# Both projections of a hybrid encoder layer: seven products of quarter matrices in place of eight

## The chip, the cores and the metric

The kernel runs on one core of a Trainium2 chip. The metric is the device time of one execution in microseconds (us). The matrix engine (TensorE) is called PE below, the vector engine DVE, the activation engine ACT, GpSimd POOL, and SP is the engine that issues the DMAs. A bare "512-column matmul" is one instruction with 128 contraction rows, 128 output rows and 512 output columns.

## The reference: what is computed

One layer over 2048 tokens of width 1024. Every row of x is normalised and multiplied by one input matrix of 3348 columns; four branches use slices of the result; their outputs (4 x 256 channels) go through a 1024 x 1024 output matrix, are added to x, and are normalised again.

```python
h = _rmsnorm(x, norm_w[layer])
proj = h @ w_in[layer]                       # [2048, 1024] @ [1024, 3348]
(a_h, a_b, a_c, a_z, g_q, g_k, g_v, g_lr, g_z, p_u, p_z, s_z, s_xbc, s_dt) = jnp.split(proj, split_idx, axis=-1)
y_a = _conv_mixer(a_h, a_b, a_c, a_z, ...)   # b * conv3(c * h) * silu(z)
y_b = _gla_mixer(g_q, g_k, g_v, g_lr, g_z, ...)   # gated linear attention, chunks of 64
y_c = _pool_mixer(p_u, p_z, ...)             # window means of 2, 4, 8, 16 tokens, gated
y_d = _ssd_mixer(s_xbc, s_dt, s_z, ...)      # conv4 + silu on xs, B, C, then a chunked state recurrence
mix = jnp.concatenate([y_a, y_b, y_c, y_d], axis=-1)
x = x + mix @ w_out[layer]                   # [2048, 1024] @ [1024, 1024]
return _rmsnorm(x, final_norm_w)
```

All of it is fp32. Both kernels split every fp32 operand into a rounded high part and the rest as a low part (`split`: the high part a copy on ACT, the low part a subtraction on DVE), and every product is the sum of three matmuls: high by low, high by high, low by high.

## The kernel before, in words

The tokens go in two segments of 1024, each in two halves of 512. The activations lie channel-major in SBUF (`hT[f]`, 8 tiles of 128 channels by 512 tokens for half f, high and low). Weights come in blocks: `load_w` loads a block of 128 columns by 1024 channels on SP's queue and splits it as one 128x1024 copy and one 128x1024 subtraction. `block_ch` then multiplies it with one half: `mm3` issues 8 x 3 = 24 matmuls of 512 columns into one PSUM bank. Two blocks are made token-major, 128 tokens to a bank: "kv" (values, gate ranks and time steps, 276 columns) and the gates "z" (512 columns). In segment 0 kv is made by `kv_outer`, which takes the 8 channel tiles as they arrive for four banks at a time; all else token-major by `block_tok`.

The program is one list of calls. `step` is called behind every block: it emits what `later` has queued, and advances `chunk_loop`, the chunked recurrence of two branches, by half a token tile. So the small work of a branch lies between the large blocks of the next. Per segment the order is: kv and q, B, k, xs, C (convolution and silu on DVE and ACT), then `conv_a` (four pairs of blocks) with `chunk_loop` beside it, the gates z, and the pool branch (`pool_u`, `pool_z`).

In segment 0 nothing waits for the rows' 1/rms: the products take x * norm_w, and `evac` multiplies by the rows' 1/rms (`rb`, L208, spread along the free axis by a way through DRAM, `rd`, L207) when a block leaves PSUM. Segment 1's rows are scaled when they are prepared (`prep`, L252), its 1/rms is made by `row_scale` (L229 to 237) in the middle of segment 0. The mixed outputs go to DRAM (`yd`). The last phase goes through 16 token tiles: `load_y` loads one and splits it, `project` makes 2 x 24 matmuls against the output matrix, which stays in SBUF, adds x (L785) and squares (L786), `emit` scales and stores (L796).

POOL does next to nothing before: memsets and the four small DMAs to `rd`.

```python
def mm3(o, ops):                                   # L183
    for i, (lh, ll, rh, rl) in enumerate(ops):
        pe.matmul(o, lhsT=lh, rhs=rl, start=i == 0, stop=False)
        pe.matmul(o, lhsT=lh, rhs=rh, start=False, stop=False)
        pe.matmul(o, lhsT=ll, rhs=rh, start=False, stop=i == last)
def evac(s, f, dst, o, scale=None):                # L210
    if s == 0 and scale is None:
        vec.tensor_tensor(dst, o, rb[:, f, :], ALU.mult)
```

Of the kernel before, what the change touches and what calls it, by code (L numbers as in the profile page):

```python
# [20 lines left out]
KD = D // P  # L21
CH = 64
# [7 lines left out]
NWARM = 4  # L30
WINS = (2, 4, 8, 16)

KVN = 276
KVK = (3, 3, 2)
# [3 lines left out]
BLOCKS = ([('q', 0), ('B', 0), ('B', 1), ('k', 0), ('xs', 0), ('xs', 1), ('C', 0), ('C', 1)]  # L38
          + [(n, j) for j in range(2) for n in ('a_h', 'a_c', 'a_b', 'a_z')]
          + [('p_z', j) for j in range(2)])  # L40
NBLK = len(BLOCKS)

# columns of the packed per-channel parameters
PC = {}
_n = 0
for _name, _w in (('caw', 6), ('psc', 2), ('scw', 24), ('scb', 6), ('gnw', 1), ('snw', 2),
                  ('dtb', 4), ('alog', 4), ('dsk', 4), ('iw', 2), ('icnt', 32), ('hm', 4), ('ind', 2), ('id', P), ('msk', P)):
    PC[_name] = _n
    _n += _w
# [4 lines left out]
def tile_hybrid_trunk(ctx: ExitStack, tc: tile.TileContext, xtok, xT, wkv, wch, wpu, wz, wo, pw_, nw, par, gw, fnw, out):  # L54
    nc = tc.nc
    vec, act, pe, sp = nc.vector, nc.scalar, nc.tensor, nc.sync

    cp = ctx.enter_context(tc.tile_pool(name="cp", bufs=1))
    pbig = ctx.enter_context(tc.tile_pool(name="pbig", bufs=2))
    pw = ctx.enter_context(tc.tile_pool(name="pw", bufs=4))  # L60
    px = ctx.enter_context(tc.tile_pool(name="px", bufs=2))
    pseg = ctx.enter_context(tc.tile_pool(name="pseg", bufs=1))
    pg = ctx.enter_context(tc.tile_pool(name="pg", bufs=9))
    psm = ctx.enter_context(tc.tile_pool(name="psm", bufs=2))
    dr = ctx.enter_context(tc.tile_pool(name="dr", bufs=1, space=DRAM))
# [34 lines left out]
    nc.gpsimd.memset(ones, 1.0)  # L100
# [9 lines left out]
    for t in (halo_x, halo_u, halo_p, sg):  # L110
        nc.gpsimd.memset(t, 0.0)
    sd0 = psm.tile([P, 256], F32, tag="sd", name="sd0", bufs=2)
    nc.gpsimd.memset(sd0, 0.0)
    state = dict(sd=sd0)

    yd = dr.tile([SEQ // P, P, KD, P], F32, name="yd")
    rd = dr.tile([4, HALF], F32, name="rd")
    wd = dr.tile([2, P, D], F32, name="wd")

# [1 line left out]
    def rsqrt(ssq, inv, n, v=None):  # L121
        """1/sqrt(ssq*inv + EPS) of a [128, n] tile (or 1/sqrt(v)), times RS"""
# [20 lines left out]
    def load_w(src, n):  # L143
        """one packed weight tile [128, n] in its two parts"""
        raw = pw.tile([P, 1024], F32, tag="raw", name=nm("raw"), bufs=3)[:, :n]
        sp.dma_start(raw, src)
        return split_w(raw, n)

    def split_w(raw, n):
        hi = pw.tile([P, 1024], F32R, tag="wh", name=nm("wh"))[:, :n]  # L150
        lo = pw.tile([P, 1024], F32R, tag="wl", name=nm("wl"))[:, :n]
        split(raw, hi, lo)
        return hi, lo

    def fold_pu(j):
        """p_u's projection block j with the pool's channel mixing folded into it, to wd"""
        raw = px.tile([P, KD, P], F32, tag="xT", name=nm("raw"))
        wt_ = px.tile([P, 1024], F32, tag="xT", name=nm("raw"))
        sp.dma_start(wt_, wpu[j])
        mix = gen()[:, :P]  # L160
        sp.dma_start(mix, pw_[j])

        def fold(hf):
            tp = tr()
            for i in range(4):
                k = hf * 4 + i
                pe.matmul(tp[:, i * P:(i + 1) * P], lhsT=wt_[:, k * P:(k + 1) * P],  # L167
                          rhs=mix, start=True, stop=True)
            act.copy(raw[:, hf * 4:hf * 4 + 4, :], tp.rearrange("p (a b) -> p a b", a=4))
            if hf:  # L170
                sp.dma_start(wd[j], raw.rearrange("p a b -> p (a b)"))
        later(1, lambda: fold(0))
        later(2, lambda: fold(1))

    def load_kv(tiles):
        ws = []
        for i in tiles:
            k0, n = sum(KVK[:i]), KVK[i]
            w = load_w(wkv[:, k0 * KVN:(k0 + n) * KVN], n * KVN)
            ws += [(w[0][:, c * KVN:(c + 1) * KVN], w[1][:, c * KVN:(c + 1) * KVN]) for c in range(n)]  # L180
        return ws

    def mm3(o, ops):  # L183
        """o = sum of lhsT^T rhs over (lh, ll, rh, rl), each product in its three parts"""
        last = len(ops) - 1
        for i, (lh, ll, rh, rl) in enumerate(ops):
            pe.matmul(o, lhsT=lh, rhs=rl, start=i == 0, stop=False)  # L187
            pe.matmul(o, lhsT=lh, rhs=rh, start=False, stop=False)  # L188
            pe.matmul(o, lhsT=ll, rhs=rh, start=False, stop=i == last)  # L189

    hT = {}

    def big(f):
        return (pbig.tile([P, KD, HALF], F32R, tag=f"big{f}", name=nm("bh")),
                pbig.tile([P, KD, HALF], F32R, tag=f"big{f}", name=nm("bl")))

    def square_sums(xs, ssq):
        for j, xk in enumerate(xs):
            act.activation(xk, xk, AF.Square, accum_out=ssq[:, j:j + 1])  # L199

    def scale_first(f, xs):
# [688 lines left out]
```

## Time and profile before

| what | value |
|---|---|
| time, median of 3 runs | 844.27 us (844.14 to 845.06) |
| span of the profiled execution | 844.6 us |
| PE busy | 816.5 us, 97% of the span, 4272 matmuls |
| DVE busy | 499.3 us, 59%, 1253 instructions |
| ACT busy | 275.4 us, 33% |
| POOL busy | 6.3 us, 1%, 22 instructions |
| chain that ended last, by engine | PE 86%, DMA 8%, DVE 2%, ACT 2% |
| DMA | 86.71 MB, mean 103 GB/s |

The span runs from the first to the last instruction of one profiled execution, and lies 0.3 us over the median of the timed runs. A busy time adds the durations of an engine's instructions, overlaps counted once. PE's matmuls are pipelined: the duration that a matmul shows is longer than the step from one start to the next, so that a sum of work is better made from starts than from durations. The chain that ended last is followed back from the last instruction through what released each step.

### The profile page before, as it was taken

How to read it: one execution, taken by the hardware profiler on the slowest of the kernel's cores; microseconds unless marked ns; L12 is line 12 of the kernel's file. 1: busy time of each engine (PE TensorE's matmuls, PEld its weight loads, DVE VectorE, ACT ScalarE, POOL GpSimd, SP SyncE). 2: the span in 40 equal slices, each digit the busy share in tenths (PEclk: the TensorE clock that was granted, in tenths of full speed). 3: DMA queues.
4: the chain of work that ended last, by engine and by line, in shares of the span. 5: the costliest groups of instructions: out<-in, count | busy, mean ns of one | idle time of the engine just before them, and what ended most of it. 6: DMA issues, size and time to landing. Idle time of an engine off the chain costs nothing.

```text
span 844.6 us, 11158 instructions
## 1 busy us (share of the span) xinstructions
PE 816.5 (97%) x4272; PEld 675.4 (80%) x4272; DVE 499.3 (59%) x1253; ACT 275.4 (33%) x487; POOL 6.3 (1%) x22
## 2 busy tenths in 40 slices
PE   7975999999999999999999999999999999999996
PEld 6954888787878888998888787878888888888885
DVE  5545757674754588955846464544578765555544
ACT  5633444242212332355545211213334332122211
POOL 0000000000000000000000000000000000000000
PEclk9987999999999999999999999999999999999999
DMA  8664101144741033523011102111045654443221
GB/s 283 231 158 115 47 29 51 51 148 119 117 135 38 26 116 113 190 61 125 26 51 50 50 27 75 45 44 38 25 162 165 181 191 151 150 150 124 101 100 50
DMA packets 38836, 86.71 MB, mean 103 GB/s; under 512 B 3872, under 2 KB 17536, under 8 KB 38784
## 3 DMA queue, kind: packets, MB, share of 16 engines
q1 hardware_dynamic: 38656, 86.00, 32.4%
q8 instruction: 33, 0.54, 0.3%
q14 instruction: 19, 0.16, 0.1%
q0 software_dynamic: 128, 0.01, 0.0%
HBM read 68.16 MB, written 17.83 MB: 102 GB/s over the span
## 4 chain that ended last, share of the span: by engine, by line
PE 86%; DMA 8%; DVE 2%; ACT 2%; issue 1%; SPq 1%; DVEq 0%; ACTq 0%
PE acc L187 27%; PE acc L189 27%; PE acc L188 27%; DMA xtok<-in_xtok 3%; DMA rd<-rt 2%; PE up L391 1%; PE tr L638 1%; PE oy L399 1%; PE oy L403 1%; DMA rb<-rd 1%; DMA xT<-in_xT 1%; DMA xk<-in_xtok 1%; ACT xtok L199 1%; DMA raw<-in_wkv 1%; PE tr L167 0%
## 5 line engine op out<-in xcount | busy, mean ns | idle before, releaser
L187 PE MATMUL acc<-bl,wh 128*128 128x512 f32 x640 | 255.6, 399 | 6.1 <-DVE nv L127 6.1
L189 PE MATMUL acc<-bh,wl 128*128 128x512 f32 x640 | 251.3, 393 | 0.0
L188 PE MATMUL acc<-bh,wh 128*128 128x512 f32 x640 | 251.1, 392 | 0.0
L187 PEld LDWEIGHTS acc<-bl,wh 128*128 128x128 f32 x640 | 121.3, 190 | 31.9 <-issue 6.3
L189 PEld LDWEIGHTS acc<-bh,wl 128*128 128x128 f32 x640 | 121.1, 189 | 26.0
L188 PEld LDWEIGHTS acc<-bh,wh 128*128 128x128 f32 x640 | 121.4, 190 | 23.9
L188 PE MATMUL acc<-bh,yh 128*128 128x512 f32 (+1 forms) x264 | 101.0, 383 | 0.0
L189 PE MATMUL acc<-bh,yl 128*128 128x512 f32 (+1 forms) x264 | 101.0, 383 | 0.0
L187 PE MATMUL acc<-bl,yh 128*128 128x512 f32 (+1 forms) x264 | 101.0, 383 | 0.0
L140 ACT CAST wh<-raw 128x1024 fp32r<-128x1024 f32 (+3 forms) x57 | 55.9, 982 | 119.6 <-PE acc L188 106.1
L141 DVE TENSOR_TENSOR wl<-raw,wh 128x1024 fp32r<-128x1024 f32 (+3 forms) x57 | 64.5, 1135 | 36.9 <-ACT wh L140 33.6
L187 PE MATMUL acc<-wl,bh 128*128 128x512 f32 (+1 forms) x192 | 69.0, 359 | 0.0
L189 PE MATMUL acc<-wh,bl 128*128 128x512 f32 (+1 forms) x192 | 68.5, 357 | 0.0
L188 PE MATMUL acc<-wh,bh 128*128 128x512 f32 (+1 forms) x192 | 68.4, 356 | 0.0
L376 DVE SCALAR_TENSOR_TENSOR g<-g,prm,g 128x512 f32<-128x512 f32 x72 | 53.7, 751 | 8.2 <-ACT g L374 6.7
L189 PEld LDWEIGHTS acc<-bh,yl 128*128 128x128 f32 x264 | 49.6, 188 | 9.7
L188 PEld LDWEIGHTS acc<-bh,yh 128*128 128x128 f32 x264 | 49.6, 188 | 9.7
L187 PEld LDWEIGHTS acc<-bl,yh 128*128 128x128 f32 x264 | 49.6, 188 | 9.7
L785 DVE TENSOR_TENSOR r<-acc,xk 128x512 f32<-128x512 f32 (+1 forms) x33 | 22.3, 675 | 56.2 <-PE acc L189 55.0
L786 ACT ACTIVATE xk<-r 128x512 f32<-128x512 f32 (+1 forms) x33 | 20.4, 618 | 86.8 <-issue 66.6
L187 PEld LDWEIGHTS acc<-wl,bh 128*128 128x128 f32 x192 | 36.1, 188 | 5.3 <-issue 0.3
L189 PEld LDWEIGHTS acc<-wh,bl 128*128 128x128 f32 x192 | 36.1, 188 | 5.2
(191 smaller groups left out, 872.8 us busy)
## 6 DMA issues: line engine op xcount, KB each, us to landing
raw<-in_wch SPq DMA_DIRECT2D x36, 512.0 KB, 3.4
xk<-in_xtok SPq DMA_DIRECT2D x24, 512.0 KB, 3.6
yr<-yd SPq DMA_DIRECT2D x16, 512.0 KB, 4.2
out<-ot SPq DMA_DIRECT2D x30, 256.0 KB, 2.2
xT<-in_xT SPq DMA_DIRECT2D x14, 512.0 KB, 4.4
xtok<-in_xtok SPq DMA_DIRECT2D x8, 512.0 KB, 6.4
raw<-in_wz SPq DMA_DIRECT2D x8, 512.0 KB, 3.9
yd<-g SPq DMA_DIRECT2D x16, 256.0 KB, 2.8
```

What stands on the lines that cost most here:

```text
L140: act.copy(hi, raw)
L141: vec.tensor_sub(lo, raw, hi.bitcast(F32))
L187: pe.matmul(o, lhsT=lh, rhs=rl, start=i == 0, stop=False)
L188: pe.matmul(o, lhsT=lh, rhs=rh, start=False, stop=False)
L189: pe.matmul(o, lhsT=ll, rhs=rh, start=False, stop=i == last)
L199: act.activation(xk, xk, AF.Square, accum_out=ssq[:, j:j + 1])
L376: vec.scalar_tensor_tensor(t, xin[:, k:k + 512], pcol('scw', 4 * i + k), t, ALU.mult, ALU.add)
L391: pe.matmul(o[:, CH + g * P:CH + (g + 1) * P], lhsT=bt[r, tt, g, :], rhs=wxs[r, tt, g * P:(g + 1) * P], start=True, stop=True)
L399: pe.matmul(oy[rows[i], 0:256], lhsT=q[:, tok[i]], rhs=st[i][0], start=True, stop=True)
L403: pe.matmul(oy[rows[i], 256 + g * P:256 + (g + 1) * P], lhsT=cc[:, g, tok[i]], rhs=st[i][1][:, gs], start=True, stop=True)
L785: vec.tensor_tensor(r[:, cs], o, xk[:, cs], ALU.add)
L786: act.activation(xk[:, cs], r[:, cs], AF.Square, accum_out=sq[:, i:i + 1])
```

## The change

It applies Strassen's identity in Winograd's form to both large products. Two blocks of 128 weight columns (a "pair") are taken with both halves of the tokens: the weights as a 2 x 2 matrix of quarters (two blocks by two halves of the 1024 channels), the activations as a 2 x 2 matrix of quarters (two halves of the channels by two halves of the tokens). Seven products of quarters replace eight. Every product of quarters is 4 channel tiles x 3 parts = 12 matmuls of 512 columns (`mm12`), a pair 84 (`pair7`), where it was 4 blocks x 24 = 96.

- **Weights.** `prep7` loads a pair's four quarters (128x512), makes four sums on POOL, and splits seven (ACT copy, DVE subtraction). It runs one pair ahead, a step at each `tick` of the pair before.
- **Activations.** `quarters` makes seven quarter matrices `H` of each segment: b11, b21, b22, and t1 to t4, which come from four differences each 128x2048 (`diff_quarters`), and splits them. Since the identity mixes the halves, the rows' 1/rms can't be left for the evacuation: in segment 0 `quarters` first multiplies all four quarters by `rb`.
- **Evacuation.** A pair's four results come from four banks: one ACT copy and five DVE additions with a PSUM operand. Products 3, 5 and 6 are accumulated on top of another in PSUM.
- **What stays as it was by count:** kv (now k by k in both segments, `outer4`) and the gates z; z moves from behind the pairs to ahead of them, goes to DRAM (`szd`) and is read back in `gate_outputs`.
- **Moved to POOL:** in `chunk_loop` the scaling of xs by the step weights, by `dsk`, and the spreading of the state (`sb`); in the output phase three of four additions of x.
- **Order of work:** pairs qk, B, xs, C, a_h, a_c, a_b, a_z, p_u, p_z; a pair has 7 ticks; `chunk_loop` takes 3 ticks for a token tile. All of the first segment's row scales are loaded in 16 tiles of 128x512 during kv. The next segment's activations are scaled under p_u (`next_rows`), the output matrix is loaded there in segment 1. The output phase does token tiles 0 and 1 as before, and the other 14 as seven pairs.
- **Memory.** Weight tiles come from one pool of 20 tiles of 512 columns, general tiles from 10 (9 before), `acc` has 4 PSUM banks (3 before; `oy` shares `tr`'s).

```diff
+    def prep7(load, w7):
+        a11, a12, a21, a22 = [wt("wr", F32) for _ in range(4)]
+        load(a11, a12, a21, a22)
+        yield 1
+        s1 = wt("ws", F32)
+        pool.tensor_add(s1, a21, a22)
+        s2 = wt("ws", F32)
+        pool.tensor_sub(s2, s1, a11)
+        yield 1
+        w7.append(split_w(s2))
+        yield 1
+        pool.tensor_sub(a21, a11, a21)
+        w7.append(split_w(a11))
+        yield 1
+        w7.append(split_w(a21))
+        s4 = wt("ws", F32)
+        pool.tensor_sub(s4, a12, s2)
...
+    def mm12(o, w, h, start, cs=slice(0, 512)):
+        (wh, wl), (hh, hl) = w, h
+        for k in range(KH):
+            ks = slice(k * P, (k + 1) * P)
+            for i, (a, b) in enumerate(((wh, hl), (wh, hh), (wl, hh))):
+                pe.matmul(o[:, cs], lhsT=a[:, ks], rhs=b[:, k, cs], start=start and k == 0 and i == 0,
...
+    def pair7(w7, H, ev11, d12, d21, d22, done):
+        b = acc()
+        mm12(b, w7[0], H['t2'], True)
+        tick()
+        a = acc()
+        mm12(a, w7[1], H['b11'], True)
+        act.copy(d21, a)
+        vec.tensor_tensor(d12, b, d21, ALU.add)
+        tick()
+        c = acc()
+        mm12(c, w7[2], H['t3'], True)
+        vec.tensor_tensor(d22, c, d12, ALU.add)
+        tick()
+        mm12(a, w7[3], H['b21'], False)
+        ev11(a)
+        tick()
+        d = acc()
+        mm12(d, w7[4], H['t1'], True)
+        vec.tensor_tensor(d22, d, d22, ALU.add)
+        tick()
+        mm12(c, w7[5], H['t4'], False)
+        vec.tensor_tensor(d21, c, d12, ALU.add)
+        done(0)
+        tick()
+        mm12(d, w7[6], H['b22'], False)
+        vec.tensor_tensor(d12, d, d12, ALU.add)
+        done(1)
...
+    def diff_quarters(B, ks):
+        b11, b12, b21, b22 = [b[:, ks, :] for b in B]
+        vec.tensor_sub(b11, b12, b11)
+        vec.tensor_sub(b12, b22, b12)
+        vec.tensor_sub(b22, b22, b11)
+        vec.tensor_sub(b21, b21, b22)
...
+    def row_scale(hf, rt):
+        for j in range(4):
+            for h in range(2):
+                xk = gen("xk")[:, :512]
+                sp.dma_start(xk, xtok[hf * 4 + j][:, h * 512:(h + 1) * 512])
+                act.activation(xk, xk, AF.Square, accum_out=ssq[:, j, h:h + 1])
...
         def update(tt):
+            wx = psm.tile([P, 4, CH], F32, tag="wx", name=nm("wx"), bufs=2)
+            pool.tensor_tensor(wx, x4, wt_[:, tt, :].unsqueeze(2).to_broadcast([P, 4, CH]), ALU.mult)
+            pool.tensor_tensor(x4, x4, pcol('dsk', 0, 4).unsqueeze(2).to_broadcast([P, 4, CH]), ALU.mult)
...
-            vec.tensor_tensor(sb, sg.unsqueeze(1).to_broadcast([P, 4, CH]),
-                              pcol('hm', 0, 4).unsqueeze(2).to_broadcast([P, 4, CH]), ALU.mult)
+            pool.tensor_tensor(sb, sg.unsqueeze(1).to_broadcast([P, 4, CH]),
+                               pcol('hm', 0, 4).unsqueeze(2).to_broadcast([P, 4, CH]), ALU.mult)
...
+    def next_rows(s):
+        for f in range(2):
+            rb = row_scale_bc(2 * s + f)
+            for h in range(2):
+                raw = quarter(f, h)
+                for k in range(0, KH, 2):
+                    sp.dma_start(raw[:, k:k + 2, :], xT[2 * s + f, :, h * KH + k:h * KH + k + 2, :])
+                    for c in (k, k + 1):
+                        vec.scalar_tensor_tensor(raw[:, c, :], raw[:, c, :], nwt[:, h * KH + c:h * KH + c + 1], rb,
...
+        def quarters():
+            H = {}
+            if s == 0:
+                for f in range(2):
+                    rb = row_scale_bc(f)
+                    for h in range(2):
+                        for k in range(0, KH, 2):
+                            r = quarter(f, h)[:, k:k + 2, :]
+                            vec.tensor_tensor(r, r, rb.unsqueeze(1).to_broadcast([P, 2, HALF]), ALU.mult)
+                H['b11'], H['b21'] = [split_quarter(quarter(0, h)) for h in range(2)]
+                H['b22'] = split_quarter(quarter(1, 1))
+            else:
+                H['b11'], H['b21'], H['b22'] = std[0, 0], std[0, 1], std[1, 1]
...
+            for k in range(0, KH, 2):
+                diff_quarters(B, slice(k, k + 2))
+            for n, r in (('t2', B[3]), ('t3', B[1]), ('t1', B[0]), ('t4', B[2])):
+                H[n] = split_quarter(r)
...
+        for f in range(2):
+            o = [acc() for _ in range(4)]
+            if f == 1:
+                H = quarters()
+            outer4([std[f, 0], std[f, 1]], wzt, 512, o)
+            for i in range(4):
+                z = gen("z")[:, :512]
+                if i % 2:
+                    vec.tensor_copy(z, o[i])
+                else:
+                    act.copy(z, o[i])
+                sp.dma_start(szd[s * TT + f * 4 + i], z)
...
+        def done(j):
+            if j == 0:
+                for c in range(2):
+                    pool.tensor_add(r[1][c], r[1][c], xb[c])
...
+                emit(tt + 1, r2[:, 1, :], sb_)
+            else:
+                pool.tensor_add(r[0][1], r[0][1], xa[1])
...
+        pair7(w7, H, ev11, r[0][1], r[1][0], r[1][1], done)
```

How the instructions stand on three engines at the places that matter is shown below, first before and then with the change. A row is line, operation, output<-inputs, shape, and how often it stands there in a row.

**SP's queue at the start.** Before, the kv weights (`raw<-in_wkv`) stand between the activations (`xT`), and the row tiles (`xk<-in_xtok`) behind them:

```order
L528 DMA xT_163<-in_xT 128x1024
L556 DMA raw_125<-in_wkv 128x552
L528 DMA xT_173<-in_xT 128x1024
L556 DMA raw_128<-in_wkv 128x552
L146 DMA raw_183<-in_wch 128x1024
L528 DMA xT_189<-in_xT 128x1024
L539 DMA xk_196<-in_xtok 128x1024
```

With the change the last two of the eight kv tiles (`wr<-in_wkv`) stand behind both halves of the activations and among the 16 row tiles:

```order
L296 DMA xk_507<-in_xtok 128x512
L709 DMA wr_187<-in_wkv 128x276
L296 DMA xk_510<-in_xtok 128x512
L296 DMA xk_513<-in_xtok 128x512
L296 DMA xk_516<-in_xtok 128x512
L296 DMA xk_519<-in_xtok 128x512
L296 DMA xk_522<-in_xtok 128x512
L709 DMA wr_193<-in_wkv 128x276
L714 DMA wr_552<-in_wz 128x512
```

So the last kv tile, which the first four PSUM banks need, moved behind everything else that the start loads.

**DVE ahead of the first blocks of segment 0.** Before, the first channel-major block (q) leaves its bank behind one weight split:

```order
L206 TENSOR_SCALAR rt<-ny_311 128x4
L624 TENSOR_SCALAR kv_386<-kv_386,rt 128x276 x4
L141 TENSOR_TENSOR wl_573<-raw_570,wh_572 128x1024
L215 SCALAR_TENSOR_TENSOR q_388<-acc_400,rb 128x512
L127 TENSOR_SCALAR nv_365<-ssq_358 128x4
```

With the change, between the gates of the first half (`z_778`) and the first pair stand the row scaling (L792), the splits (L152) and the differences (L267 to L270) of the quarters, and behind these rows four more lines of splits, x2 each:

```order
L812 COPY z_778<-acc_603 128x512
L792 TENSOR_TENSOR xq_115<-xq_115,rb_785 128x1024 x2
L792 TENSOR_TENSOR xq_161<-xq_161,rb_785 128x1024 x2
L792 TENSOR_TENSOR xq_362<-xq_362,rb_795 128x1024 x2
L792 TENSOR_TENSOR xq_376<-xq_376,rb_795 128x1024 x2
L152 TENSOR_TENSOR hl_807<-xq_115,hh_806 128x1024 x2
L152 TENSOR_TENSOR hl_814<-xq_161,hh_813 128x1024 x2
L152 TENSOR_TENSOR hl_821<-xq_376,hh_820 128x1024 x2
L267 TENSOR_TENSOR xq_115<-xq_362,xq_115 128x1024 x2
L268 TENSOR_TENSOR xq_362<-xq_376,xq_362 128x1024 x2
L269 TENSOR_TENSOR xq_376<-xq_376,xq_115 128x1024 x2
L270 TENSOR_TENSOR xq_161<-xq_161,xq_376 128x1024 x2
```

The first pair's own weight splits stand behind all 30 of these 128x1024 instructions.

**POOL under the chunk recurrence.** Before, POOL's whole list between the start and segment 1 is memsets and small DMAs:

```order
L298 MEMSET rst_606 96x512
L207 DMA rd<-rt 128x4x1 x2
L328 MEMSET g_666 128x8
L328 MEMSET g_676 128x8
L237 DMA rd<-ny_1649 128x4x1
L237 DMA rd<-ny_1679 128x4x1
L298 MEMSET rst_3211 96x512
```

With the change the weight sums of the next pair (L194 to L205) and the recurrence's own scalings (L421, L422, L453) stand in one line:

```order
L421 TENSOR_TENSOR wx_1874<-xs_980,wt_209 128x256
L422 TENSOR_TENSOR xs_980<-xs_980,prm 128x256 x2
L205 TENSOR_TENSOR ws_1676<-wr_1571,ws_1595 128x512
L194 TENSOR_TENSOR ws_1822<-wr_1795,wr_1796 128x512
L196 TENSOR_TENSOR ws_1824<-ws_1822,wr_1793 128x512
L200 TENSOR_TENSOR wr_1795<-wr_1793,wr_1795 128x512
L453 TENSOR_TENSOR sb_1778<-sg,prm 128x256
L421 TENSOR_TENSOR wx_1985<-xs_980,wt_209 128x256
L422 TENSOR_TENSOR xs_980<-xs_980,prm 128x256
L453 TENSOR_TENSOR sb_1786<-sg,prm 128x256
L205 TENSOR_TENSOR ws_1930<-wr_1794,ws_1824 128x512
```

POOL went from memsets to 129 additions of 128x512 and 64 multiplications of 128x256, all with SBUF operands.

## Rows read from the trace of the kernel before

**Rows 1.** Busy time by stretch, with count, granted PE clock, DMA share and rate.

```profile
core 0: us, PE busy (x) PEld busy (x) DVE busy (x) ACT busy (x) POOL busy (x), PEclk, DMA share, GB/s
0.00:20.00 20.00, 14.97 (x88) 12.84 (x89) 12.16 (x21) 11.35 (x17) 1.70 (x12) 1.00 0.81 279
20.00:40.00 20.00, 20.00 (x141) 18.97 (x140) 12.47 (x32) 14.06 (x24) 0.94 (x1) 1.00 0.75 263
0.00:80.00 80.00, 59.92 (x317) 51.30 (x318) 41.09 (x100) 39.51 (x64) 3.55 (x16) 0.89 0.67 205
80.00:836.60 756.60, 756.26 (x3956) 624.00 (x3955) 454.66 (x1141) 235.41 (x422) 2.78 (x6) 1.00 0.29 92
836.60:844.60 8.00, 0.27 (x3) 0.07 (x1) 3.57 (x13) 0.51 (x2) 0.00 (x0) 0.80 0.19 66
```

**Rows 2.** Groups of instructions by line and form, PE: busy us, mean ns.

```profile
L187 PE MATMUL acc<-bl,wh 128*128 128x512 f32 x640 | 255.6, 399 | 6.1 <-DVE nv L127 6.1
L187 PE MATMUL acc<-bl,yh 128*128 128x512 f32 x248 | 96.5, 389 | 0.0
L187 PE MATMUL acc<-wl,bh 128*128 128x512 f32 x128 | 50.4, 394 | 0.0
L187 PE MATMUL acc<-bl,yh 128*128 128x256 f32 x16 | 4.5, 283 | 0.0
```

**Rows 3.** The same view of PE, from 0 to 80 us.

```profile
L187 PE MATMUL acc<-bl,wh 128*128 128x512 f32 x36 | 16.2, 450 | 6.1 <-DVE nv L127 6.1
L572 PE MATMUL up<-wh,bl 128*128 128x276 f32 x32 | 9.0, 289 | 0.0
```

**Rows 4.** Timeline of PE in the output phase: start us, us, instruction.

```profile
680.00 0.39 PE L187 MATMUL acc<-bl,yh 128*128 128x512 f32 x1
...
704.93 0.39 PE L189 MATMUL acc<-bh,yl 128*128 128x512 f32 x1
```

**Rows 5.** Timeline of PE at the start, 276 columns.

```profile
12.99 0.29 PE L572 MATMUL acc<-wh,bh 128*128 128x276 f32 x1
...
14.50 0.29 PE L572 MATMUL acc<-wh,bh 128*128 128x276 f32 x1
```

**Rows 6.** Groups by line and form, DVE.

```profile
L141 DVE TENSOR_TENSOR wl<-raw,wh 128x1024 fp32r<-128x1024 f32 x48 | 58.6, 1223 | 35.4 <-ACT wh L140 32.3 <-PE tr L638 2.6
```

**Rows 7.** Timeline of DVE under the pool branch of segment 0.

```profile
326.37 0.75 DVE L492 SCALAR_TENSOR_TENSOR g<-g,prm,g 64x512 f32<-64x512 f32 x1
327.04 0.68 DVE L213 TENSOR_TENSOR g<-acc,rb 128x512 f32<-128x512 f32 x1
...
336.02 0.69 DVE L480 TENSOR_TENSOR g<-g 128x514 f32<-128x514 f32 x1
336.62 0.69 DVE L141 TENSOR_TENSOR bl<-hf,bh 128x512 fp32r<-128x512 f32 x1
...
343.46 1.29 DVE L141 TENSOR_TENSOR bl<-hf,bh 128x512 fp32r<-128x512 f32 x2
```

**Rows 8.** Timeline of POOL, whole span.

```profile
343.64 0.52 POOL L298 MEMSET rst<- 96x512 f32 x1 [134.23 <-DVE g L492]
```

**Rows 9.** Chain that ended last, at the start: start us, us, what.

```profile
55.59 9.84 DMA rd<-rt
65.45 5.83 DMA rb<-rd
```

**Rows 10.** The same chain in the steady part.

```profile
94.93 0.44 PE tr L638 x4
...
208.19 1.09 PE tr L167 x8
...
472.94 0.65 PE up L391 x8
...
485.99 0.65 PE up L391 x8
```

**Rows 11.** Timeline of ACT beside the branch a_c of segment 0.

```profile
198.02 1.06 ACT L199 ACTIVATE xtok<-xtok 128x1024 f32<-128x1024 f32 x1 [8.66 <-DMA xtok<-in_xtok]
```

More of the change, by code (lines that the diff above doesn't have):

```diff
@@ L30 @@
 NWARM = 4
+NW = 20
+NG = 10
+TPT = 3
 WINS = (2, 4, 8, 16)
 KVN = 276
-KVK = (3, 3, 2)
 OFF = dict(a_h=0, a_b=256, a_c=512, a_z=768, q=1024, k=1152, v=1280, lr=1536, g_z=1552,
            p_u=1808, p_z=2064, s_z=2320, xs=2576, B=2832, C=3088, dt=3344)
-BLOCKS = ([('q', 0), ('B', 0), ('B', 1), ('k', 0), ('xs', 0), ('xs', 1), ('C', 0), ('C', 1)]
-          + [(n, j) for j in range(2) for n in ('a_h', 'a_c', 'a_b', 'a_z')]
-          + [('p_z', j) for j in range(2)])
+PAIRS = ('qk', 'B', 'xs', 'C', 'a_h', 'a_c', 'a_b', 'a_z', 'p_u', 'p_z')
+BLOCKS = [b for n in PAIRS if n != 'p_u' for b in ((('q', 0), ('k', 0)) if n == 'qk' else ((n, 0), (n, 1)))]
 NBLK = len(BLOCKS)
@@ L99, in tile_hybrid_trunk @@
     ones = cp.tile([P, 1], F32, name="ones")
-    nc.gpsimd.memset(ones, 1.0)
+    pool.memset(ones, 1.0)
     def pcol(name, i=0, n=1):
@@ L141, in split, with split_w @@
         vec.tensor_sub(lo, raw, hi.bitcast(F32))
[L143 to L151, printed above, removed]
+    def split_w(raw, n=512):
+        hi, lo = wt("wh")[:, :n], wt("wl")[:, :n]
         split(raw, hi, lo)
         return hi, lo
[L155 to L189, printed above, removed]
@@ L776, in project @@
[L776 to L786 removed]
+        if s:
+            wk = [load_kv(k) for k in range(KD)]
@@ new lines, in tile_hybrid_trunk, with more @@
+        w7 = []
+        drain(prep7(load_pair(PAIRS[0]), w7))
+        for n, name in enumerate(PAIRS):
+            w_next = []
+            if n + 1 < len(PAIRS):
+                prep_[0] = prep7(load_pair(PAIRS[n + 1]), w_next)
+            if name == 'a_h':
+                chunks[0] = chunk_loop(kv, kt, q, aG, aD, bt, xs, wt_, cc, after_chunks)
+                if s + 1 < NSEG:
+                    later(1, lambda: fold_pu(0))
+                    later(6, lambda: fold_pu(1))
+            if name == 'a_c' and s + 1 < NSEG:
+                later(1, lambda: row_scale(2 * s + 2, psm.tile([P, 4], F32, tag="rt2", name=nm("rt2"))))
+                later(5, lambda: row_scale(2 * s + 3, psm.tile([P, 4], F32, tag="rt2", name=nm("rt2"))))
+            if name == 'p_u':
+                nxt = next_rows(s + 1) if s + 1 < NSEG else next_wout()
+                def more(g=nxt):
+                    if next(g, 0):
+                        later(1, more)
+                later(2, more)
+            if name == 'p_z':
+                later(6, lambda: std_half(0))
+            pair7(w7, H, *consumers(name))
+            if prep_[0] is not None:
+                drain(prep_[0])
+                prep_[0] = None
+            w7 = w_next
```

863 lines of the change are left out of this document (441 added, 422 removed).

## The prediction

> **What bounds the kernel now.** I read the busy times by stretch first: from 80 to 836.6 us PE works 756.26 of 756.60 us, at full granted clock, and DVE 454.66 [rows 1]. So the middle is PE's, and a matmul taken out there is worth its step. The step comes from PE's timeline: from 680.00 to 704.93 us lie 110 steps, 0.2266 us each [rows 4]; the 0.39 us that a row shows overlaps the next. A 276-column matmul takes (14.50 - 12.99) / 12 = 0.126 us [rows 5]. The groups by form give the counts, each for one of the three parts: 640 + 248 + 128 of 512 columns and 16 of 256, so 3 x 1016 + 24 = 3072 in 512-column terms [rows 2]. The first 80 us are not PE's: there stand 36 + 36 + 35 matmuls of 512 columns (three lines alike) and 192 of 276 (the row and its like) [rows 3], 24.2 + 24.2 us, and some 0.7 of small ones. So PE idled 31 us there, the last of it behind the 1/rms on its way through DRAM, 9.84 and 5.83 us [rows 9]. Behind the last matmul lie 8 us [rows 1].
>
> **The change, part by part.**
>
> *Matmuls removed.* A pair has 84 for 96. There are 20 pairs and 7 in the output phase, so 27 x 12 = 324 go; kv, gates and small products keep their number. 324 x 0.2266 = **-73.4 us**, all from PE's full stretch, if nothing else ends last.
>
> *DVE.* Additions with independent operands start 0.60 us apart (336.02, 336.62), scaled ones 0.67 (326.37, 327.04) [rows 7]; a 128x1024 one takes 1.22 [rows 6], less the same overlap 1.14. A pair costs DVE 5 additions out of PSUM and 7 splits, 12 x 0.60 = 7.2 us, and its branch's own work. By the order of instructions that makes 9.8 us for qk, 15.0 B, 16.4 xs, 16.4 C, 14.3 a_h, against 84 x 0.2266 = 19.0 of PE. From a_c to p_u it is 20.3 + 25.0 + 17.2 + 29.3 = 91.8, since the recurrence comes on top, and in p_u 16 scalings of the next segment (16 x 0.67 = 10.7). PE has there 76.1, 5 2/3 token tiles of recurrence and folds. A token tile is 485.99 - 472.94 = 13.05 less 48 x 0.2266, 2.17 us, so 12.3; eight times four transposes of 0.44 in all are 3.5; folds 2 x 1.09 = 2.2 [rows 10]: together 94.1. So DVE is level with PE there, with 2 us to spare in segment 0. In segment 1 (no folds, no row scaling of four halves) it is 83 against 92, 9 to spare. Averages hide p_u, 29.3 against 19.0, and weights are split only one pair ahead: **+10** (0 if earlier slack covers it, 20 if a_b does the same).
>
> *Start.* The last kv tile stands behind 9.6 MB (activations and rows, 4.2 each, and kv 1.1). At 279 and 263 GB/s [rows 1] that takes 35 us, with landing some 41 (an estimate), so the first kv half ends near 42 and the second, 12 us of PE each, near 55; four gate blocks (96 x 0.2266 = 21.8) end near 77. Their banks leave behind the decay chain on DVE, some 8 us, so the second gates end near 107. Meanwhile, from about 89, DVE does 30 instructions of 128x1024 x 1.14 = 34 us, with the first pair's splits behind: its first matmul comes near 125. PE has done 24.2 + 43.5 + 2 = 70 by then and idled 55, 24 more than before: **+24**. With quarters begun as soon as gates end it would be 13; with each wait 4 us longer, 36.
>
> *Segment 1's start.* Behind p_u DVE has 34.7 us of splits and scalings to the kv weights, while PE has p_z and half of kv, 31.1: 3.7. The second half waits for 8 splits of 1.14, half of it covered: 4.5. **+8** (0 to 15).
>
> *Output.* Seven quarters must be built while four standard blocks run (96 x 0.2266 = 21.8): 8 differences and 8 splits of 1.14, 18.2, behind other splits: **+5** (0 to 8). Each of its pairs then costs DVE 12.5 against 19.0.
>
> *ACT.* The row scales of segment 1 go through ten general tiles, of which a_c holds eight. Before, ACT stood 8.66 us for such a tile [rows 11]; I take half, **+4** (0 to 10).
>
> *POOL.* No tensor operation with inputs runs on POOL before. Its price has ends: a memset of 96x512, which passes the data once, takes 0.52 us [rows 8]; three passes would be 1.57. I take 1.0. From a_c to p_u, both segments, there are 32 of 128x512 and 48 of half the size (0.55): 58 us, beside 184 of PE, so POOL alone is no bound. What counts is whether it stops DVE. At 343.64 the memset began inside a DVE subtraction with two SBUF inputs, and two of these took 1.29 in all, their usual time [rows 7, 8]: one pass, a write, cost nothing. An addition has two reads besides. So 2/3 of 58 = 39 us could collide, by two thirds of DVE's time there (the rest reads PSUM): 25, less the 11 to spare: **+14**. The ends are 0 and 58 - 11 = 47.
>
> *Tail.* The last tile's addition now runs on POOL, and the emission stands behind it: **+3** (2 to 5).
>
> *Nothing for:* the row squares on ACT, gates through DRAM (0.25 MB each, loaded ticks ahead; without that cover 3 us a tile), chunk scalings that leave DVE (in its sums already).
>
> Sum: -73.4 + 24 + 10 + 8 + 5 + 4 + 14 + 3 = -5.4. Against this execution's span, 844.6, that is 839.2; the median lies 0.3 lower: **839 us**.
>
> A rule that would change the first term: the Trainium skill, "TensorE: Matmul & The Clock Gate", "Back-to-back issue gap", gives a sustained 131 ns for a 512-column matmul. By it the 324 are worth 42 us and the sum is 870. The trace differs: 0.2266 us at full granted clock, 110 times in a row [rows 4], so the row decides.
>
> **Rivals.**
>
> *A: POOL stops nobody and DVE evens itself out* (the terms +14 and +10 vanish): 815. For it, the memset that cost nothing [rows 8]; against it, that a memset reads no operand, and DVE is level with PE over four pairs. 0.18.
>
> *B, slower: POOL and DVE exclude each other.* Each POOL operation stops the DVE's instructions with two SBUF inputs for its whole time, and p_u, a_b and the kv splits become DVE's. The price is 58 - 11 = 47 in place of 14: 872; if instructions that read PSUM run on meanwhile, 39 - 11 = 28: 853. It decides from the point where the collisions take 19 us more than DVE has to spare (14 + 5.4). For it: 32 + 48 operations, all with SBUF operands, in a stretch where DVE has 11 us in 186. Against it: the memset's row [rows 7, 8]. 0.32. The Trainium skill, "SBUF — State Buffer", "SBUF: two separate sides", says just this: the port pair that the two share is "an exclusive lock, not a bandwidth split", for a GpSimd operation that reads SBUF against a DVE one with two SBUF inputs. The memset, which reads nothing, falls outside that rule, and so no row here contradicts it.
>
> *C: the products don't shrink as counted*, because alternating banks and 12-matmul groups lengthen the step; 2748 at 0.23 in place of 0.2266 cost 9 us: 848. The order of instructions shows 84 per pair, so the count stands. 0.04.
>
> **How the numbers follow.** The forecast has 0.46. Its own range, the unknowns but POOL's partly at either end, is 824 to 856. A measurement of this kernel tells 0.2%, 1.7 us, from no change. Of the forecast, 0.28 lies below 842.6, 0.07 within 1.7 us of 844.3 and 0.11 above; A is faster, 0.18; B slower, 0.31 of 0.32; C 0.02 each way. Faster 0.49, same 0.08, slower 0.43. Both signs being likely, the range goes to 810 (A with the start at 19) and to 878 (B with the start at 30): about 0.06 is left out below and 0.1 above.
>
> **What would show it.** The matmul count falls to 2748 in 512-column terms with steps of 0.227. The first matmul of a pair comes at 125 us; at 112 or 140 the start term is wrong. POOL's 128x512 additions show their time beside 1.0. If B is right, DVE's 0.69 us additions grow towards 1.7 where a POOL addition overlaps, and PE's idle time before products of a_b, a_z and p_u is ended by DVE, 28 to 47 us in all; if A is right, PE's middle is as full as before. The forecast is wrong if PE's idle time behind 125 us, tail aside, is under 20 or over 65 us.

## The result, and the profile after

The changed kernel takes 919.25 us (917.48 to 920.72) against 844.2 us: 1.0892 times, interval 1.0863 to 1.0921. Forecast were 839 us, with a range to 878. The profiled execution has a span of 915.4 us.

Busy time by stretch of the changed kernel (columns as in [rows 1]):

```profile
120.00:160.00 40.00, 26.36 (x101) 20.79 (x102) 28.34 (x37) 16.74 (x25) 8.20 (x7) 0.75 0.22 73
280.00:320.00 40.00, 30.89 (x194) 23.29 (x194) 33.52 (x113) 13.89 (x35) 10.51 (x10) 0.87 0.32 95
800.00:840.00 40.00, 32.93 (x136) 25.79 (x135) 31.22 (x64) 12.30 (x27) 14.42 (x11) 0.96 0.41 138
```

Where [rows 1] had a full PE from 80 us on, PE now waits in every part: the first pair, the recurrence, the output pairs. No other engine is full there either (DVE 28 to 34 of 40 us): POOL and DVE share the work, and the experiments show that they hold each other up. The granted clock falls in the same stretches (0.75 to 0.96, where [rows 1] had 1.00).

The groups by line and form, POOL and DVE, of the changed kernel:

```profile
L205 POOL TENSOR_TENSOR ws<-wr,ws 128x512 f32<-128x512 f32 x27 | 41.4, 1532 | 52.0 <-issue 41.9 <-DVE wl L152 7.2 <-PE acc L221 2.6
L194 POOL TENSOR_TENSOR ws<-wr,wr 128x512 f32<-128x512 f32 x27 | 37.4, 1384 | 370.1 <-PE acc L285 124.8 <-DMA wr<-in_wch 82.0 <-PE acc L221 70.9
L453 POOL TENSOR_TENSOR sb<-sg,prm 128x256 f32<-128x256 f32 x32 | 21.7, 677 | 57.9 <-DVE sg L451 34.0 <-PE oy L439 20.2 <-DVE na L145 1.8
L962 POOL TENSOR_TENSOR r<-r,xk 128x512 f32<-128x512 f32 x14 | 18.6, 1342 | 67.5 <-DVE r L243 64.2 <-DVE r L246 3.3
L545 DVE SCALAR_TENSOR_TENSOR t<-xin,prm,t 128x512 f32<-128x512 f32 x72 | 68.6, 985 | 4.4 <-ACT t L543 4.1
L143 DVE SCALAR_TENSOR_TENSOR na<-ny,sq 128x1 f32<-128x1 f32 x48 | 25.8, 537 | 1.6
```

In these groups a POOL addition of 128x512 takes 1.34 to 1.53 us (forecast 1.0). Before L205 POOL stood 41.9 us for nothing that the profile shows ("issue"); what ended that, no run here shows. On the other side, the convolution's scaled addition on DVE takes 985 ns, where one of that size took 0.75 us [rows 7], and one of a single element a partition 537 ns (218 in e1 below). One instance shows why. POOL's timeline in the output phase:

```profile
790.65 1.29 POOL L194 TENSOR_TENSOR ws<-wr,wr 128x512 f32<-128x512 f32 x1 [1.33 <-DMA wr<-yd]
792.63 1.29 POOL L966 TENSOR_TENSOR r<-r,xk 128x512 f32<-128x512 f32 x1 [0.70 <-DVE ny L147]
```

and DVE's, of the same stretch:

```profile
790.68 0.15 DVE L140 TENSOR_SCALAR ny<-na 128x1 int32<-128x1 int32 x1
790.87 1.08 DVE L143 SCALAR_TENSOR_TENSOR na<-ny,sq 128x1 f32<-128x1 f32 x1
791.88 0.68 DVE L250 TENSOR_TENSOR r<-acc,r 128x512 f32<-128x512 f32 x1
792.48 0.14 DVE L147 SCALAR_TENSOR_TENSOR ny<-na,ny 128x1 f32<-128x1 f32 x1
792.66 1.28 DVE L143 SCALAR_TENSOR_TENSOR na<-ny,sq 128x1 f32<-128x1 f32 x1
```

Each L143 (two SBUF inputs, one element a partition) ends when the POOL addition ends, 790.65 + 1.29 = 791.94 and 792.63 + 1.29 = 793.92. L140 with one input ran its 0.15 us inside the first. L147 has two inputs too; at 792.48, with POOL idle, it took 0.14 us.

PE's timeline of the changed kernel: the first pair, the start of the first output pair (742.64), and two later places in the output pairs:

```profile
125.91 0.80 PE L221 MATMUL acc<-hl,wh 128*128 128x512 f32 x1 [16.77 <-DVE hl L152]
...
742.64 0.80 PE L221 MATMUL acc<-hl,wh 128*128 128x512 f32 x1 [8.37 <-ACT wh L151]
743.23 0.63 PE L221 MATMUL acc<-hh,wl 128*128 128x512 f32 x1
743.66 0.63 PE L221 MATMUL acc<-hl,wh 128*128 128x512 f32 x1
...
786.76 0.50 PE L221 MATMUL acc<-hl,wh 128*128 128x512 f32 x1 [2.58 <-DVE r L243]
787.10 0.40 PE L221 MATMUL acc<-hh,wh 128*128 128x512 f32 x1
787.34 0.40 PE L221 MATMUL acc<-hh,wl 128*128 128x512 f32 x1
...
833.17 0.80 PE L221 MATMUL acc<-hl,wh 128*128 128x512 f32 x1 [2.59 <-DVE r L243]
833.76 0.63 PE L221 MATMUL acc<-hh,wh 128*128 128x512 f32 x1
834.19 0.63 PE L221 MATMUL acc<-hh,wl 128*128 128x512 f32 x1
```

The first pair comes at 125.9 us, forecast was 125. After the wait of 8.37 us PE restarts with steps of 0.43 us (743.23 to 743.66), where [rows 4] has 0.2266; the granted clock is 0.50 from 743 to 747 us, the lower of its two levels, for about ten matmuls. Not every wait is followed by this: behind 786.76 the steps are 0.24 at a granted clock of 1.00, behind 833.17, after a wait as long, 0.43 at 0.50. The wait for L243 recurs in the output pairs: product 7 adds to a bank that DVE has still to read, and DVE is late.

PE's steps from start to start, sorted from the traces (us). The first column is the count of large matmuls times 0.2266 us (512 columns) or 0.126 us (276 columns). What a step has beyond that stands under "waits" if it is over 0.35 us, under "slow steps" from 0.1 to 0.35, and under "ragged" below; small products are given with what PE waited behind them:

| | matmuls at full step | waits | slow steps | small products | ragged | both ends |
|---|---|---|---|---|---|---|
| before | 744.5 | 3.4 | 6.9 | 72.8 | 7.7 | 9.3 |
| changed | 671.1 | 108.5 | 37.4 | 76.7 | 8.5 | 13.2 |
| best version (e12 below) | 671.1 | 55.9 | 27.3 | 61.0 | 8.7 | 11.7 |

The 324 matmuls gave their 73.4 us; 105 more of waits and 30 more of slow steps took nearly twice that.

### The profile page after: what moved, and what is told of

Read it like the earlier page. It is cut to its first block, busy times and chain, and to the rows that moved or that the text cites. A ratio compares the mean times of both kernels' runs of the same rounds, so it can differ in the third digit from the quotient of the medians.

```text
span 915.4 us, 11628 instructions
## 1 busy us (share of the span) xinstructions
PE 790.2 (86%) x3924; PEld 639.2 (70%) x3924; DVE 692.7 (76%) x1425; ACT 377.5 (41%) x740; POOL 231.0 (25%) x211
## 5 line engine op out<-in xcount | busy, mean ns | idle before, releaser
L221 PE MATMUL acc<-hl,wh 128*128 128x512 f32 x788 | 322.1, 409 | 49.1 <-DVE hl L152 16.8
L221 PE MATMUL acc<-hh,wl 128*128 128x512 f32 x788 | 314.5, 399 | 4.6 <-DVE wl L152 4.6
L221 PE MATMUL acc<-hh,wh 128*128 128x512 f32 x788 | 314.1, 399 | 0.0
L221 PEld LDWEIGHTS acc<-hl,wh 128*128 128x128 f32 x788 | 152.6, 194 | 89.4 <-DVE hl L152 17.2
L221 PEld LDWEIGHTS acc<-hh,wl 128*128 128x128 f32 x788 | 152.2, 193 | 38.1 <-DVE wl L152 5.1
L221 PEld LDWEIGHTS acc<-hh,wh 128*128 128x128 f32 x788 | 152.6, 194 | 30.1
L194 POOL TENSOR_TENSOR ws<-wr,wr 128x512 f32<-128x512 f32 x27 | 37.4, 1384 | 370.1 <-PE acc L285 124.8
L152 DVE TENSOR_TENSOR wl<-wr,wh 128x512 fp32r<-128x512 f32 (+1 forms) x144 | 99.0, 692 | 35.0 <-ACT wh L151 24.6
L285 PE MATMUL acc<-wh,hh 128*128 128x276 f32 (+1 forms) x256 | 87.0, 376 | 25.3 <-ACT wh L151 17.6
L285 PE MATMUL acc<-wl,hh 128*128 128x276 f32 (+1 forms) x256 | 94.6, 371 | 4.7 <-DVE wl L152 4.7
L152 DVE TENSOR_TENSOR wl<-ws,wh 128x512 fp32r<-128x512 f32 x81 | 61.1, 754 | 43.0 <-ACT wh L151 38.6
L285 PE MATMUL acc<-wh,hl 128*128 128x276 f32 (+1 forms) x256 | 92.9, 365 | 0.0
L152 DVE TENSOR_TENSOR hl<-xq,hh 128x1024 fp32r<-128x1024 f32 (+1 forms) x56 | 65.0, 1197 | 11.0 <-ACT hh L151 10.9
L205 POOL TENSOR_TENSOR ws<-wr,ws 128x512 f32<-128x512 f32 x27 | 41.4, 1532 | 52.0 <-issue 41.9
```

The lines of the kernel that those rows point to most:

```text
L152: vec.tensor_sub(lo, raw, hi.bitcast(F32))
L194: pool.tensor_add(s1, a21, a22)
L205: pool.tensor_sub(s4, a12, s2)
L221: pe.matmul(o[:, cs], lhsT=a[:, ks], rhs=b[:, k, cs], start=start and k == 0 and i == 0, stop=k == KH - 1 and i == 2, skip_group_check=True)
L285: pe.matmul(o[tt][:, :n], lhsT=a[:, k % KH, sl], rhs=wts[k][b], start=k == 0 and i == 0, stop=k == KD - 1 and i == 2)
```

## Experiments

The theories: **L**, POOL operations that read SBUF and DVE instructions with two SBUF inputs exclude each other, and DVE made late is what PE waits for; **S**, DVE has too much work of its own, whatever POOL does. Comparisons are with the kernel before on the same chip, which took 846.7 us beside e1 to e4, 843.1 beside e5 to e8 and 843.7 beside e9 to e12. So differences between runs with different bases are given by their ratios, 0.01 being 8.4 us. The base itself moved by 3 us, so some 3 us of such a difference stay open; where the traces show the place of a gain, its size there is given too.

**e1_no_pool.** All of POOL's tensor work to DVE.

```diff
-        pool.tensor_add(s1, a21, a22)
+        vec.tensor_tensor(s1, a21, a22, ALU.add)
```
(and so for all 193 operations)

> All 193 tensor operations of POOL are given to DVE (weight sums, the recurrence's scalings, the residual additions). In the changed kernel's trace POOL is busy 231 us with them. Theory L (a POOL operation and a DVE instruction with two SBUF inputs exclude each other, and the time behind the first pair is DVE made late by POOL): DVE gets 129 x 0.60 + 64 x 0.33, some 99 us more, but loses 231 us of stops; the mean of DVE's 128x512 scaled additions of the convolution (985 ns in the changed kernel) falls back to 750, and the time falls from 919 to 880 to 900. Theory S (DVE has too much work of its own, whatever POOL does): half of the 99 us comes on the path, 950 to 970, and the convolution's additions stay near 985.

Measured 889.06 us, 1.0502 (1.0484 to 1.052); the convolution's additions:

```profile
L545 DVE SCALAR_TENSOR_TENSOR t<-xin,prm,t 128x512 f32<-128x512 f32 x72 | 51.4, 748 | 2.9 <-ACT t L543 2.7
```

DVE has 99 us more to do (the expectation's estimate), and the kernel is 0.039 faster, 33 us. L holds in its direction, but not in its price. DVE's busy time grows only from 692.7 to 707.0 us, so POOL had stretched DVE's instructions by some 85 us (99 less 14, an estimate), not by all of POOL's 231.

**e2_sums_dve.** Only the weight sums to DVE (the diff above, four lines).

> Only the four weight sums of each pair (108 operations of 128x512, 155 us of POOL) go to DVE, 65 us more there. Theory L: 890 to 905, most of what all of POOL's work costs. Theory S: 935 to 955.

Measured 881.85 us, 1.0405 (1.0381 to 1.043), better than either theory said (L: 890 to 905) and than e1: the sums are what hurt.

**e3_rest_dve.** The reverse: the recurrence's scalings and the residual additions to DVE, the sums stay.

```diff
-            pool.tensor_tensor(wx, x4, ...
+            vec.tensor_tensor(wx, x4, ...
-                    pool.tensor_add(r[1][c], r[1][c], xb[c])
+                    vec.tensor_tensor(r[1][c], r[1][c], xb[c], ALU.add)
```
(and so for the other scalings of the recurrence, `sb` among them, and the third addition)

> Only the recurrence's scalings and the residual additions go to DVE (64 operations of 128x256 and 21 of 128x512, 76 us of POOL), 34 us more there; the weight sums stay on POOL. Theory L: 900 to 912, the output pairs' step falls from 23.3 us towards 20. Theory S: 925 to 935, the output pairs' step stays at 23.3 or grows.

Measured 926.0 us, 1.0942 (1.0916 to 1.0968). S's number: with the sums still on POOL, more work on DVE brings nothing, and rather costs (the intervals touch). But L's other sign came too: the output pairs' step fell from some 23.4 us to 21.5 to 22.3. By the traces the output pairs are 10 us shorter, and from a_c to p_z, where the recurrence now runs on DVE, both segments together are 10 us longer. So the edit mixes a gain and a loss, and decides between neither theory.

**e4_no_sums.** No weight sums at all.

```diff
-        s1 = wt("ws", F32)
-        pool.tensor_add(s1, a21, a22)
-        s2 = wt("ws", F32)
-        pool.tensor_sub(s2, s1, a11)
+        s1, s2 = a21, a12
```

> The weight sums are left out: the seven splits take the loaded quarters as they are, so the products are those of other matrices. PE, DVE and ACT keep their instruction counts. Theory L: the time of the collisions with the sums comes back without DVE's extra 65 us, 865 to 885. Theory S: DVE's work is the same, 910 to 919.

Measured 864.48 us, 1.0204 (1.0165 to 1.0244). So the sums on POOL cost 1.0892 - 1.0204 = 0.069, 58 us, on DVE 1.0405 - 1.0204, 17 us.

**e5_memset.** POOL as busy, but reading nothing.

```diff
-        pool.tensor_add(s1, a21, a22)
+        for _ in range(3):
+            pool.memset(s1, 1.0)
```

> Each of the four weight sums on POOL is replaced by three memsets of the same 128x512 tile, so POOL is as busy (3 x 0.45 to 0.52 us in place of 1.4 us) and hands over as late, but reads nothing; the products are those of other matrices. Theory R (only a POOL operation that reads SBUF stops DVE): near the run without sums, 860 to 875, and the convolution's scaled additions on DVE near 750 ns. Theory B (any POOL operation stops DVE, or the late hand-over is what costs): 905 to 920, the additions near 985.

Measured 868.06 us, 1.0297 (1.0272 to 1.0322). Its groups of POOL and DVE:

```profile
L195 POOL MEMSET ws<- 128x512 f32 x81 | 42.8, 528 | 142.6 <-DVE wl L152 50.1 <-PE acc L289 46.5 <-PE acc L225 45.0
...
L549 DVE SCALAR_TENSOR_TENSOR t<-xin,prm,t 128x512 f32<-128x512 f32 x72 | 52.8, 768 | 4.4 <-ACT t L547 4.1
```

Three of these take 1.58 us, longer than an addition, and DVE's addition is back at 768 ns. POOL's time and late hand-over cost 0.009, 8 us, against e4; its reading the other 50 of the 58.

The pages of the changed kernel and of e5 show it on DVE. POOL is equally busy and DVE has the same 1425 instructions, but they take 57 us less:

```profile
PE 790.2 (86%) x3924; PEld 639.2 (70%) x3924; DVE 692.7 (76%) x1425; ACT 377.5 (41%) x740; POOL 231.0 (25%) x211
PE 775.6 (90%) x3924; PEld 630.4 (73%) x3924; DVE 636.0 (74%) x1425; ACT 378.9 (44%) x740; POOL 233.3 (27%) x427
```

The two traces also show where the time went, from a pair's first addition out of PSUM to the next pair's (us):

| stretch | changed | e5 | difference |
|---|---|---|---|
| start to qk of segment 0 | 143.4 | 141.0 | 2.4 |
| qk to a_h, both segments | 178.0 | 166.6 | 11.4 |
| a_h to a_c, both segments | 49.3 | 52.8 | -3.5 |
| a_c to p_z, both segments | 222.9 | 211.4 | 11.5 |
| p_z to qk of segment 1, p_z to the output pairs | 158.0 | 149.4 | 8.6 |
| first to last output pair | 140.5 | 121.1 | 19.4 |
| behind | 23.2 | 22.0 | 1.2 |

**e6_start.** On e2: the quarters' scaling, first splits and differences ahead of the gates; gates leave PSUM on ACT.

```diff
+        for k in range(0, KH, 2):
+            diff_quarters(B, slice(k, k + 2))
         for f in range(2):
             o = [acc() for _ in range(4)]
-            if f == 1:
-                H = quarters()
...
+        for n, r in (('t1', B[0]), ('t4', B[2])):
+            H[n] = split_quarter(r)
```

> On top of the weight sums on DVE (881.9 us): the row scaling, the first splits and the differences of the quarters are emitted ahead of the gates instead of between their two halves, and the gates leave PSUM on ACT alone. If the idle time before the first pair is DVE's 34 us of quarters standing behind the first half's gates, the first matmul of a pair comes at 108 to 115 us instead of 126, and the time falls by 8 to 18 us, to 864 to 874, some of it from segment 1. If the chain of row scales through DRAM is what is late, the first matmul stays at 126 and the time within 4 us of 882.

Measured 863.24 us, 1.024 (1.0215 to 1.0265), 0.0165 or 14 us less than e2. The first matmul of a pair came only at 122.5, so that part missed; what went were the waits within the first pair and its slow steps: its first evacuation came at 129.8 us against 143.2.

**e7_kv1.** On e2: five kv weight tiles of segment 1 split under p_z.

```diff
+                if s + 1 < NSEG:
+                    wk = []
+                    for k in range(5):
+                        later(2 + k, lambda k=k: wk.append(load_kv(k)))
```

> On top of the weight sums on DVE (881.9 us): five of the eight kv weight tiles of segment 1 are loaded and split under the pair p_z instead of behind it. If kv's weight splits are what PE waits for there (gaps of 1.9 us before four of the eight channel tiles, each followed by matmuls at half clock), the first qk evacuation of segment 1, 104 us behind that of p_z, comes 6 to 12 us earlier and the time is 870 to 876. If the splits only move the queue on DVE, within 3 us of 882.

Measured 873.36 us, 1.0353 (1.0333 to 1.0372), 0.005 or 4 us less than e2 by the ratios. In the traces the stretch from p_z's first addition out of PSUM to qk's of segment 1 is 95.2 us, in e2 104.3: 9 us, as forecast, and 873 lies in the forecast 870 to 876. PE's waits before kv tiles, in e2:

```profile
396.90 0.39 PE L285 MATMUL acc<-wl,hh 128*128 128x276 f32 x1 [1.99 <-DVE wl L152]
400.66 0.40 PE L285 MATMUL acc<-wl,hh 128*128 128x276 f32 x1 [1.89 <-DVE wl L152]
404.43 0.60 PE L285 MATMUL acc<-wl,hh 128*128 128x276 f32 x1 [1.79 <-DVE wl L152]
```

In the trace the steps behind the first two of these waits are 0.13 us, so only the third is followed by the half clock that the expectation names. In e7 the longest wait before a kv tile is 1.33 us, at 398.26.

**e8_resid.** On e2: the residual additions to DVE, the recurrence's stay on POOL.

```diff
-                    pool.tensor_add(r[1][c], r[1][c], xb[c])
+                    vec.tensor_tensor(r[1][c], r[1][c], xb[c], ALU.add)
```

> On top of the weight sums on DVE (881.9 us): the 21 residual additions go to DVE too, the recurrence's scalings stay on POOL. The output pairs step at 20.1 us with the additions on POOL, at 19.2 to 19.9 without any POOL work: theory L says 875 to 879; theory S (DVE gets 13 us more) 884 to 890.

Measured 868.96 us, 1.03 (1.0275 to 1.0325), 0.0105 or 9 us less than e2, more than L's 3 to 7; in the traces 9 us of it lie in the output pairs, whose step is 19.2 to 20.0. The recurrence is a bargain on POOL: moved too (e1) it costs 0.020, 17 us. Its operations are half as long (0.67 to 0.82 us in e8), and no other addition of POOL's is left beside them; which of the two makes it cheap was not tested.

**e9_all3.** e6, e7 and e8 together.

> The three cures together on top of the weight sums on DVE: quarters ahead of the gates, five kv tiles of segment 1 under p_z, residual additions on DVE. If they work at different places their gains add: 881.9 - 18.6 - 8.5 - 12.9 = 842, between 838 and 848. If they feed on the same idle time (DVE's queue as a whole), 850 to 858.

Measured 845.27 us, 1.0016 (1.0001 to 1.0032): the three gains add (0.032 by themselves, 0.039 together; in the traces 14 us at the start, 12 at segment 1's, 8 in the output pairs), and the change is about level with the kernel before.

**e10_out.** e9, and the first output pair's weights prepared under the standard blocks.

```diff
         if c == 1:
+            prep_[0] = prep7(load_rows(2), w7)
```

> The three cures, and the first output pair's weights prepared under the standard blocks instead of behind them. PE stood 8 to 9 us before the first output pair, and restarted at half clock: 6 to 11 us less than the run with the three cures. If DVE is full there (differences and splits of the output matrix), no change.

Measured 845.64 us, 1.0011 (0.9989 to 1.0034). No change: the wait before that pair is 7.6 us, in e9 8.7. DVE is busy for all of the 18 us before it (675 to 693 us), with the splits of the quarters ahead of the weight sums, so the wait is DVE's queue.

**e11_rows.** e9, with segment 1's row scales under a_h, the folds under a_b.

```diff
-            if name == 'a_c' and s + 1 < NSEG:
+            if name == 'a_h' and s + 1 < NSEG:
                 later(1, lambda: row_scale(...
```

> The three cures, and the row scales of segment 1 read under a_h instead of a_c, the folds under a_b. If ACT, waiting for row tiles behind the general tiles that a_c holds, is what makes a_h to a_b 29 us a pair in segment 0 against 22.5 to 24 in segment 1, these pairs get 4 to 8 us shorter together, with the time. If the folds and the recurrence are it, within 3 us of the run with the three cures.

Measured 846.24 us, 1.0022 (1.0001 to 1.0043). No change. But the edit moved ACT's wait for row tiles and did not remove it (from 190 to 320 us 12.9 us in e11, 11.0 in e9), so what makes these pairs long, and whether the term of 4 us exists, stays open.

**e12_kvfirst.** e9, with segment 0's kv weights loaded ahead of the row tiles, into general tiles.

```diff
+        for k in range(k0, k1):
+            sp.dma_start(kvr[k], wkv[:, k * KVN:(k + 1) * KVN])
         prep_first(0, k0, k1, n)
-        wk += [load_kv(k) for k in range(k0, k1)]
+        wk += [split_w(kvr[k], KVN) for k in range(k0, k1)]
```

> The three cures, and the eight kv weight tiles of segment 0 loaded ahead of the row tiles and of the second half's activations, as in the kernel before. The gap of 10 us at 41 us goes. If the start is bound by the loads, the first pair and the end come 5 to 10 us earlier; if by DVE's quarters or by the way of the row scales through DRAM, which the loads put later by 2 us, the end stays within 3 us.

Measured 836.19 us, 0.9906 (0.9875 to 0.9938): 0.9% faster than the kernel before. PE in e9:

```profile
40.44 1.29 PE L285 MATMUL acc<-wh,hh 128*128 128x276 f32 x4 [10.31 <-ACT wh L151]
...
122.02 0.39 PE L221 MATMUL acc<-hl,wh 128*128 128x512 f32 x1
```

and in e12:

```profile
48.78 0.79 PE L285 MATMUL acc<-wh,hh 128*128 128x512 f32 x1 [7.14 <-ACT kv L778]
...
111.08 0.39 PE L221 MATMUL acc<-hl,wh 128*128 128x512 f32 x1
```

The first pair comes 11 us earlier and the end 9: the loads' order was the start's bound, once DVE was out of its way. The gap of 10.31 us is gone; a wait of 7.14 us now stands ahead of the gates, whose banks ACT has still to empty of kv. In e12 DVE is still full in a stretch (busy times, columns as in [rows 1]):

```profile
320.00:360.00 40.00, 33.30 (x143) 26.38 (x143) 40.00 (x73) 17.04 (x33) 1.28 (x4) 0.87 0.33 97
```

That is p_u and p_z of segment 0, where the forecast saw DVE as the bound.

## Why the prediction was wrong

- **Matmuls removed, -73.4:** right. The count fell by 324, and the step held (180 in a row at 0.2268 us).
- **POOL, +14: the step that failed.** Three things in it.
  - The premise. A memset that DVE did not notice [rows 7, 8] was taken as one pass of an addition's three, so that a third of the time was free. e5 shows that memsets say nothing of additions: with 233 us of POOL busy and no sums, DVE's instructions are 57 us shorter in all and the span 51.
  - The place. The term counts only the pairs a_c to p_u, 32 of 108 sums, and puts POOL at nothing elsewhere. There the sums cost 11.5 us, near the 14; but 11.4 lie in qk to C, 8.6 at the borders of the segments and 19.4 in the output pairs. B and xs take 23.2 and 24.8 us from first evacuation to first evacuation (20.1 and 21.1 in e2), the output pairs 23.2 to 23.6 (19.2 to 20.0 in e8). In all the sums cost 58 us, the residual additions 9 more with the sums gone.
  - The price of one. 1.0 us, the middle of two ends, was 1.38 (L194) to 1.53 (L205); the upper end, 1.57, was near.
- **Rival B** named the mechanism, given 0.32. Its sign at its place did not come: PE's idle time from a_h to p_u is 9.1 us in segment 0 and 2.9 in segment 1, not 28 to 47. And its price, each POOL operation's whole time, is too high: 155 us of sums stretched DVE by 57. The forecast's own sign of being wrong did come: PE is idle 74 us behind 125.9 us, over its 65.
- The Trainium skill, "SBUF — State Buffer", "SBUF: two separate sides", has the rule that the prediction quoted for B, that one engine waits for the other's whole instruction. The trace agrees where it can be seen: an L143 of one element waits out a POOL addition, 1.08 and 1.28 us. The Trainium skill, "GPSIMD Engine Reference", "3. Performance versus the Vector engine", gives a ratio of 1.96 for an addition of 2048 elements; by the 0.69 us of DVE that is an estimate of 1.35 us, and the rows have 1.34 to 1.53. The prediction did not use it.
- **A term left out: slow steps.** Many waits of PE are followed by steps at the lower clock; 30 us more than before. The forecast priced waits by their length alone.
- **Start, +24:** right for its sign, the first matmul of a pair (125.9 us). But the first pair then waits 3.1 and 4.6 us more for its weights and runs at the lower clock, so its first evacuation comes 17.5 us behind its first matmul, in e6 7.3: 10 us that the term does not have. e6 and e12 take the first pair to 122.5 and 111.1: DVE's quarters and the order of the loads, the two parts of the term.
- **Segment 1's start, +8:** the place was right; e7 gives 4 back by the ratios, 9 in the traces, and waits are left there.
- **DVE's unevenness, +10, and output, +5:** not told apart by a run. The first output pair waits 8.4 us, and e10 did not move it.
- **ACT, +4:** open (e11). **Tail, +3:** 12.0 us behind the last matmul's start against 8.0, near.
- **The other rivals:** A's condition, POOL stopping nobody, is what e5 comes nearest to: 868, not 815. e6 to e8, on e2, take 0.032, 27 us, from what remained there; the rest is open. C fell: the step is 0.2268 where PE runs on.
- **The miss is 80 us** (919 against 839). The sums and the residual additions cost 67, 53 more than the term; 10 lie in the first pair. The other 17, and how far these parts overlap, no run tells apart.

## What to carry to other kernels

Before giving elementwise work to POOL, ask what DVE does meanwhile: if DVE's instructions there read two SBUF operands, POOL's additions are paid for twice, on POOL and on DVE. Here 108 sums cost 58 us on POOL and 17 on DVE; the recurrence's short operations, with the sums gone, were 17 us cheaper on POOL. Ask it of every stretch, not only of the fullest. Fewer matmuls are worth their step only while the engines that feed PE keep up, and a wait can cost its length and a slow restart. A row of a different operation (a write for a read) is no lower bound.

## What the runs showed of the hardware

A DVE instruction of one element per partition and two SBUF inputs (L143) takes 1.08 and 1.28 us instead of 0.22 where it meets a POOL addition, and ends with it. Over the kernel, 155 us of POOL additions stretched DVE's instructions by 57 us. POOL memsets of the same tiles (0.53 us each, 324 of them) leave DVE's scaled additions near where they were (768 ns, 748 without any POOL work). After a wait of 8.4 us PE ran about ten 512-column matmuls at steps of 0.43 us (granted clock 0.50); after waits of 2.6 us it did so at 833.17 us and not at 786.76. In the changed kernel 249 steps are lengthened by 0.1 to 0.35 us, before 44.
